# Order of work at three places of an encoder block: weights' splits behind the fourth row's norm, second product's operands behind the last group's first copy, and the last two rows' final norm

## The chip, the cores and the metric

The kernel runs on one core of a Trainium2 chip. The metric is device time of one execution in microseconds (us). Times of the trace are counted from the start of the span, the stretch that the profiler records.

## The reference

The input x is 1024 tokens by 1024 features, all in float32. What is computed:

```python
xn = _rmsnorm(h, norm_mix_w[l])
proj = xn @ w_in[l]                       # 1024 x 2832
...
h = h + jnp.concatenate([attn, gdn], axis=-1) @ w_out[l]
hn = _rmsnorm(h, norm_ffn_w[l])
h = h + jnp.square(jax.nn.relu(hn @ w_ffn_in[l])) @ w_ffn_out[l]   # 4096 inner columns
...
return _rmsnorm(h, norm_final_w)
```

`attn` is windowed attention of 8 heads, `gdn` a gated delta rule in both directions of 4 heads. The change touches the start (first norm and the first columns of `w_in`), the passage from the feed-forward block's first product to its second, and the final norm.

## The kernel before, in words

**Precision.** A float32 operand is split into two fp32r parts, hi and lo: ACT casts it to hi (L123, L1193), and POOL (L124) or DVE (L1194) subtracts hi from it for lo. A product is then three matmuls (`mm3`, L136 hi by hi, L137 hi by lo, L138 lo by hi). L numbers are lines of the kernel; in the changed kernel the same lines have numbers 1 or 2 higher from L214 on, and in the tail other ones, which are named where they matter.

**Buffers.** Tiles come from pools of a few rotating buffers, and the letters in front of a tile's name are its pool: `pg`, `dbl`, `pt`, `wr`, `wh`, `wl`, `sc` in SBUF, `psA` and `psB` of four banks each in PSUM. The numbers behind it (pt_8560) tell apart the tiles of a pool.

**Who sets the order.** Each engine works through one queue in order. The order in the queues is made when the program is built, by a scheduler that simulates the engines. Two instructions on different engines are tied by semaphores where one needs the other's data or buffer. `behind([...])` (L127) ties everything that is built in its scope to come after the given instructions in the queue of the engine that each of them is on; it adds no semaphore.

**Start.** For each row block of 128 tokens (`norm_rows`, L213 to L215) ACT squares and sums the row, POOL makes the reciprocal root in two steps (L200, L201), and DVE multiplies the row by it. PE transposes the first four blocks (L219); ACT and DVE scale the transposed parts by the norm's weight and split them (L224, L225). `proj_ab` casts a narrow weight (L291 on ACT, L292 on POOL, L293 and L296 on DVE) and gives PE its first real matmuls (L302, L303). The weights of the next projection `k` are split behind it (L123, L124).

**Feed-forward, first product.** It runs in 16 groups of 256 inner columns (`pair_products`). A group uses a scheme of seven products, P1 to P7, in place of eight; each is 12 matmuls of 128x512 here. P1, P6, P5, P7, P3, P4 share banks: P6 is accumulated onto P1's bank, after ACT has copied P1 out (L1106, `copied`); P3 onto P5's, after DVE has read that one (`add_to`, L1101); P4 onto P7's, after DVE has read that. Relu and Square are on ACT (L1111, L1112). DVE makes four sums of the results (L1162 to L1170), and all seven are stored to memory from ACT's queue (L1117).

**Second product.** It takes the same seven in the order of `SECOND`: P1, P2, P6, P5, P7, P3, P4, for each of four ranges of inner columns. `second_operands` prepares one: SP loads the left sides (L1192), ACT casts them (L1193) and DVE makes lo (L1194); of the weights DVE makes the sums T1, T2 (L1201, L1203), T3 and N4 (L1206, L1207), and ACT and POOL split them (L123, L124). In the last group the operands of the second product's first steps are prepared while the first product still runs: `prepare(0)` behind that group's P2, further ones behind P6 and P3, through `prepare_behind`:

```python
def prepare_behind(i):
    with self.behind(last_split):
        prepare(i)
```

`last_split` are the casts and subtractions of the last group's own weights, on ACT and POOL.

**Tail.** In the last range the rows are finished as P3 and P4 come out: `finish` squares a row on ACT (L1269), makes the reciprocal root on POOL and weighs the row on DVE by root and weight in one operation (L1272), then stores it (L1273). The last row, 7, is finished in halves by `finish_last` (L1253 to L1263): the upper half's Square and weighing (POOL, L1254) don't need the last matmuls, the lower half's do (L1255 to L1257).

Of the kernel before, what the change touches and what calls it, by code (L numbers as in the profile page):

```python
# [12 lines left out]
BF16 = mybir.dt.bfloat16  # L13
AF = mybir.ActivationFunctionType
ALU = mybir.AluOpType
AX = mybir.AxisListType

P = 128
# [50 lines left out]
def run(gen):  # L69
    for _ in gen:  # L70
        pass
# [7 lines left out]
class Block:  # L79
# [118 lines left out]
    def rstd(self, ss, out):  # L198
        nc = self.nc
        nc.gpsimd.tensor_scalar(out=ss, in0=ss, scalar1=1.0 / D, scalar2=EPS, op0=ALU.mult, op1=ALU.add)  # L200
        nc.gpsimd.tensor_tensor(out=out, in0=ss, in1=self.nhalf_exp[:, :1], op=ALU.pow)  # L201

    def load_x(self, t):
        x = self.pg((P, D))
# [3 lines left out]
    def norm_rows(self, x, dst=None):  # L208
        nc = self.nc
        ss, rs = self.small((P, 1)), self.small((P, 1))  # L210
        xs = dst if dst is not None else x
        scr = self.pt((P, D), BF16)
        nc.scalar.activation(out=scr, in_=x, func=AF.Square, accum_out=ss)  # L213
        self.rstd(ss, rs)  # L214
        nc.vector.tensor_scalar(out=xs, in0=x, scalar1=rs, scalar2=None, op0=ALU.mult)  # L215
        return xs

    def transpose_row(self, row, i, ps, k):
# [884 lines left out]

    def copied(self, ps):
        t = self.pt()
        self.nc.scalar.copy(out=t, in_=ps)  # L1106
        return t

    def act(self, c):
# [108 lines left out]
    def second_products(self, n, p, left, right, banks, last):  # L1218

        nc = self.nc  # L1220
        bank, tag = {"P1": ("a", "psA"), "P2": ("b", "psB"), "P5": ("c", "psB"), "P7": ("d", "psA"), "P6": ("a", None),
                     "P3": ("c", None), "P4": ("d", None)}[p]
        lo, hi = slice(0, HALF), slice(HALF, D)
        for i in range(4):
            ps = banks[bank, i] = self.ps(tag) if tag else banks[bank, i]
            tk = slice(i * P, (i + 1) * P)
            for k in range(4):
                self.mm3(ps, left[k][:, 0, tk], left[k][:, 1, tk], right[k][:, 0], right[k][:, 1],
                         tag is not None and k == 0, k == 3, tag is None)
            u2 = self.u2[i // 2][:, i % 2]  # L1230
            if p == "P6" and n == 0:
                nc.scalar.copy(out=u2, in_=ps)
                continue
            dst = {"P1": self.h[i][:, lo], "P2": self.h[i][:, lo], "P6": u2, "P5": self.h[4 + i][:, hi],
                   "P7": self.h[4 + i][:, hi], "P3": self.h[i][:, hi], "P4": self.h[4 + i][:, lo]}[p]
            if p == "P4" and last and i == 3:
                self.finish_last(7, ps)
                continue
            nc.vector.tensor_tensor(out=dst, in0=dst, in1=ps, op=ALU.add)  # L1239
            if last and p == "P6":  # L1240
                for d in (self.h[i][:, hi], self.h[4 + i][:, hi], self.h[4 + i][:, lo]):
                    nc.gpsimd.tensor_tensor(out=d, in0=d, in1=u2, op=ALU.add)
            if last and p in ("P3", "P4"):
                self.finish(i if p == "P3" else 4 + i)

    def finish_last(self, t, ps):

        nc = self.nc
        lo, hi = slice(0, HALF), slice(HALF, D)
        h = self.h[t]  # L1250
        ss, rs = self.small((P, 2)), self.small((P, 1))
        scr, hw, o = self.pt((P, HALF), BF16), [self.pt(), self.pt()], [self.pt(), self.pt()]
        nc.scalar.activation(out=scr, in_=h[:, hi], func=AF.Square, accum_out=ss[:, 1:2])  # L1253
        nc.gpsimd.tensor_tensor(out=hw[1], in0=h[:, hi], in1=self.w_fin[:, hi], op=ALU.mult)  # L1254
        nc.vector.tensor_tensor(out=h[:, lo], in0=h[:, lo], in1=ps, op=ALU.add)  # L1255
        nc.scalar.activation(out=scr, in_=h[:, lo], func=AF.Square, accum_out=ss[:, 0:1])
        nc.vector.tensor_tensor(out=hw[0], in0=h[:, lo], in1=self.w_fin[:, lo], op=ALU.mult)  # L1257
        nc.vector.tensor_tensor(out=ss[:, 0:1], in0=ss[:, 0:1], in1=ss[:, 1:2], op=ALU.add)
        self.rstd(ss[:, 0:1], rs)
# [2 lines left out]
        for i, sl in enumerate((lo, hi)):  # L1262
            (nc.scalar, nc.sync)[i].dma_start(out=self.io["out"][0, t * P:(t + 1) * P, sl], in_=o[i])  # L1263

    def finish(self, t):
        nc = self.nc
        ss, rs = self.small((P, 1)), self.small((P, 1))
        scr = self.pt((P, D), BF16)
        nc.scalar.activation(out=scr, in_=self.h[t], func=AF.Square, accum_out=ss)  # L1269
        self.rstd(ss, rs)  # L1270
        o = self.wr((P, D))
        nc.vector.scalar_tensor_tensor(out=o, in0=self.h[t], scalar=rs, in1=self.w_fin, op0=ALU.mult, op1=ALU.mult)  # L1272
        nc.sync.dma_start(out=self.io["out"][0, t * P:(t + 1) * P, :], in_=o)  # L1273

# [21 lines left out]
    def phases(self):  # L1296
# [11 lines left out]
        for half in range(2):  # L1308
            rows = [self.norm_rows(xs[4 * half + i]) for i in range(4)]
            self.xt.append([])  # L1310
            if half == 0:
                self.transpose_first(rows, self.w_mix, self.xt[half])
                next(ab)
            else:
                run(weave((itertools.islice(k, 2), 10.4),
                          (self.transpose_split(rows, self.w_mix, "psB", self.xt[half]), 4.0)))
                next(ab)
        run(ab)
        run(k)
# [45 lines left out]
            ops[i] = self.second_operands(n, w2[n], p)  # L1365

        def prepare_behind(i):
            with self.behind(last_split):
                prepare(i)

        def after_p6():
# [52 lines left out]
```

## Time and profile before

| what | value |
|---|---|
| median of 3 runs | 1226.01 us (1224.49 to 1228.44) |
| the profiled execution | 1226.09 us |
| its span | 1224.0 us |
| mean granted clock of PE | 0.989 |
| busy: PE, DVE, ACT, POOL | 96%, 70%, 50%, 46% of the span |
| DMA | 187.62 MB, mean 153 GB/s |

A row of the timeline gives the start, the duration, the engine, the line, the operation, the tile written and the tiles read, the shape, and the count where like rows are joined. In brackets stands how long the engine had been idle before it, and what ended that. PE's matmuls are pipelined: a row lasts longer than the step to the next one, and it is the steps that count. PE is the matmul, PEld the weight load beside it, SPq and ACTq are DMAs issued from those queues.

### The profile page before, as it was taken

How to read it: one execution, taken by the hardware profiler on the slowest of the kernel's cores; microseconds unless marked ns; L12 is line 12 of the kernel's file. 1: busy time of each engine (PE TensorE's matmuls, PEld its weight loads, DVE VectorE, ACT ScalarE, POOL GpSimd, SP SyncE). 2: the span in 40 equal slices, each digit the busy share in tenths (PEclk: the TensorE clock that was granted, in tenths of full speed). 3: DMA queues.
4: the chain of work that ended last, by engine and by line, in shares of the span. 5: the costliest groups of instructions: out<-in, count | busy, mean ns of one | idle time of the engine just before them, and what ended most of it. 6: DMA issues, size and time to landing. Idle time of an engine off the chain costs nothing. (4 is left out here: it accounts for less than half of the span.)

```text
span 1224.0 us, 18445 instructions
## 1 busy us (share of the span) xinstructions
PE 1173.7 (96%) x6482; PEld 961.9 (79%) x6482; DVE 855.7 (70%) x1482; ACT 610.4 (50%) x1331; POOL 560.2 (46%) x470
## 2 busy tenths in 40 slices
PE   6999999899889999998999999999999999999997
PEld 5788878687768878887788888888878888888885
DVE  4676667993489996675855454453698796987976
ACT  6455688425376662124755454554555444344443
POOL 5354312224321233232764453635456565565695
PEclk9999999899989999999999999999999999999999
DMA  6134344433645577222144444344789534343323
GB/s 244 52 103 145 92 170 152 162 123 113 207 146 182 157 249 269 76 95 100 56 154 157 146 154 164 130 155 146 240 275 317 200 103 163 131 159 116 103 86 138
DMA packets 121629, 187.62 MB, mean 153 GB/s; under 512 B 11043, under 2 KB 64416, under 8 KB 121537
## 3 DMA queue, kind: packets, MB, share of 16 engines
q1 hardware_dynamic: 103876, 155.20, 38.4%
q10 hardware_dynamic: 17661, 31.24, 6.8%
q8 instruction: 51, 0.84, 0.3%
q14 instruction: 41, 0.34, 0.1%
HBM read 122.39 MB, written 63.49 MB: 152 GB/s over the span
## 5 line engine op out<-in xcount | busy, mean ns | idle before, releaser
L136 PE MATMUL psA<-pg,wh 128*128 128x512 f32 x416 | 165.0, 397 | 2.1 <-ACT pt L473 2.1
L138 PE MATMUL psA<-pg,wl 128*128 128x512 f32 x416 | 164.5, 395 | 0.0
L137 PE MATMUL psA<-pg,wh 128*128 128x512 f32 x416 | 164.2, 395 | 0.0
L124 POOL TENSOR_TENSOR wl<-wr,wh 128x512 fp32r<-128x512 f32 x44 | 66.8, 1540 | 156.5 <-ACT wh L123 128.7
L1194 DVE TENSOR_TENSOR pg<-pg 128x512 fp32r<-128x512 f32 x112 | 124.3, 1145 | 12.9 <-ACT pg L1193 12.9
L124 POOL TENSOR_TENSOR wh<-wr,wh 128x512 fp32r<-128x512 f32 x32 | 47.0, 1487 | 138.2 <-ACT wh L123 138.2
L1111 ACT ACTIVATE pt<-pt 128x512 f32<-128x512 f32 x64 | 40.3, 632 | 122.6 <-DVE pt L1101 122.6
L136 PE MATMUL psA<-pg,pg 128*128 128x512 f32 x256 | 98.7, 391 | 0.9 <-DVE pg L1239 0.9
L137 PE MATMUL psA<-pg,pg 128*128 128x512 f32 x256 | 99.2, 391 | 0.1
L138 PE MATMUL psA<-pg,pg 128*128 128x512 f32 x256 | 99.2, 389 | 0.0
L136 PEld LDWEIGHTS psA<-pg,wh 128*128 128x128 f32 x416 | 78.8, 190 | 19.5 <-ACT pt L473 2.4
L137 PEld LDWEIGHTS psA<-pg,wh 128*128 128x128 f32 x416 | 78.7, 189 | 17.9 <-issue 0.9
L138 PEld LDWEIGHTS psA<-pg,wl 128*128 128x128 f32 x416 | 78.7, 189 | 16.7
L124 POOL TENSOR_TENSOR pg<-wr,pg 128x512 fp32r<-128x512 f32 x48 | 73.2, 1559 | 37.9 <-ACT pg L123 37.9
L1193 ACT CAST pg<-pg 128x512 fp32r<-128x512 f32 x112 | 66.7, 620 | 36.4 <-DMA pg<-sd 31.3
L137 PE MATMUL psB<-pg,pg 128*128 128x512 f32 x192 | 74.9, 390 | 0.8 <-POOL pg L124 0.7
L136 PE MATMUL psB<-pg,pg 128*128 128x512 f32 x192 | 74.7, 389 | 0.0
L138 PE MATMUL psB<-pg,pg 128*128 128x512 f32 x192 | 74.7, 389 | 0.0
L123 ACT CAST wh<-wr 128x512 fp32r<-128x512 f32 x76 | 43.6, 623 | 52.1 <-PE psA L137 31.9
L1101 DVE TENSOR_TENSOR pt<-psB,pt 128x512 f32<-128x512 f32 x39 | 26.9, 690 | 57.6 <-PE psB L138 40.7
L1101 DVE TENSOR_TENSOR pt<-psA,pt 128x512 f32<-128x512 f32 x39 | 26.7, 689 | 51.3 <-PE psA L138 34.1
L136 PEld LDWEIGHTS psA<-pg,pg 128*128 128x128 f32 x256 | 48.0, 188 | 12.1 <-DVE pg L1239 2.1
(395 smaller groups left out, 3234.8 us busy)
## 6 DMA issues: line engine op xcount, KB each, us to landing
sd<-pt ACTq DMA_DIRECT2D x112, 256.0 KB, 2.1
pg<-sd SPq DMA_DIRECT2D x112, 256.0 KB, 2.9
wr<-in_w_ffn_in SPq DMA_DIRECT2D x32, 512.0 KB, 3.6
wr<-in_w_in SPq DMA_DIRECT2D x22, 512.0 KB, 4.2
pg<-in_x SPq DMA_DIRECT2D x16, 512.0 KB, 5.0
wr<-in_w_ffn_out SPq DMA_DIRECT2D x16, 512.0 KB, 4.7
sc<-kvd SPq DMA_DIRECT2D x14, 512.0 KB, 3.7
kvd<-pt SPq DMA_DIRECT2D x16, 256.0 KB, 2.4
```

What stands on the lines that cost most here:

```text
L123: a = nc.scalar.copy(out=h, in_=raw)
L124: b = (eng or nc.gpsimd).tensor_tensor(out=l, in0=raw, in1=h.bitcast(F32), op=ALU.subtract)
L136: nc.tensor.matmul(ps, wh, xh, start=first, stop=False, skip_group_check=onto)
L137: nc.tensor.matmul(ps, wh, xl, start=False, stop=False, skip_group_check=onto)
L138: return nc.tensor.matmul(ps, wl, xh, start=False, stop=last, skip_group_check=onto)
L1101: self.nc.vector.tensor_tensor(out=out, in0=in0, in1=in1, op=ALU.add)
L1111: self.nc.scalar.activation(out=c, in_=c, func=AF.Relu)
L1193: nc.scalar.copy(out=s[:, 0], in_=raw)
L1194: v.tensor_tensor(out=s[:, 1], in0=raw, in1=s[:, 0].bitcast(F32), op=ALU.subtract)
```

## The change

There are three parts.

1. **Start.** `norm_rows` keeps its Square, its power and its multiplication (`self.normed`). Those of the fourth row block are what `proj_ab`'s first piece (its casts) and the first two pieces of the projection `k` (its weights' splits) are now built behind, on ACT, POOL and DVE.
2. **Last group.** `copied` keeps its copy (`self.moved`), and `prepare_behind` puts the preparation behind that as well: `prepare(0)` behind the copy of the last group's P1, the next ones behind the copy of its P6.
3. **Tail.** Row 7's upper half is squared and weighed (`finish_hi`) ahead of row 6's finish. Row 6 is weighed by the weight alone (L1288 of the changed kernel), and multiplied by its root later, on ACT behind the Square of row 7's lower half (L1270); its store is issued there.

```diff
     def norm_rows(self, x, dst=None):
...
+        s = nc.scalar.activation(out=scr, in_=x, func=AF.Square, accum_out=ss)
+        p = self.rstd(ss, rs)
+        m = nc.vector.tensor_scalar(out=xs, in0=x, scalar1=rs, scalar2=None, op0=ALU.mult)
+        self.normed = [s.ins, p, m.ins]
...
     def copied(self, ps):
         t = self.pt()
-        self.nc.scalar.copy(out=t, in_=ps)
+        self.moved = self.nc.scalar.copy(out=t, in_=ps).ins
...
+            if last and p == "P4" and i == 2:
+                self.finish_hi(7)
             if last and p in ("P3", "P4"):
-                self.finish(i if p == "P3" else 4 + i)
+                self.finish(i if p == "P3" else 4 + i, p == "P4" and i == 2)
+
+    def finish_hi(self, t):
+
+        nc = self.nc
+        hi = slice(HALF, D)
+        h = self.h[t]
+        self.fs, self.fhi, scr = self.small((P, 2)), self.pt(), self.pt((P, HALF), BF16)
+        nc.scalar.activation(out=scr, in_=h[:, hi], func=AF.Square, accum_out=self.fs[:, 1:2])
+        nc.gpsimd.tensor_tensor(out=self.fhi, in0=h[:, hi], in1=self.w_fin[:, hi], op=ALU.mult)
 
     def finish_last(self, t, ps):
...
         nc.vector.tensor_tensor(out=h[:, lo], in0=h[:, lo], in1=ps, op=ALU.add)
-        nc.scalar.activation(out=scr, in_=h[:, lo], func=AF.Square, accum_out=ss[:, 0:1])
+        square = nc.scalar.activation(out=scr, in_=h[:, lo], func=AF.Square, accum_out=ss[:, 0:1])
+        late, late_rs, late_t = self.late
+        with self.tc.issue_after(square.ins):
+            nc.scalar.activation(out=late, in_=late, func=AF.Copy, scale=late_rs)
+        nc.sync.dma_start(out=self.io["out"][0, late_t * P:(late_t + 1) * P, :], in_=late)
...
         o = self.wr((P, D))
+        if weigh_first:
+            nc.vector.tensor_tensor(out=o, in0=self.h[t], in1=self.w_fin, op=ALU.mult)
+            self.late = o, rs, t
+            return
...
             if half == 0:
+                first = self.normed
                 self.transpose_first(rows, self.w_mix, self.xt[half])
-                next(ab)
+                with self.behind(first):
+                    next(ab)
             else:
-                run(weave((itertools.islice(k, 2), 10.4),
-                          (self.transpose_split(rows, self.w_mix, "psB", self.xt[half]), 4.0)))
+                with self.behind(first):
+                    run(weave((itertools.islice(k, 2), 10.4),
+                              (self.transpose_split(rows, self.w_mix, "psB", self.xt[half]), 4.0)))
...
         def prepare_behind(i):
-            with self.behind(last_split):
+            with self.behind(last_split + [self.moved]):
                 prepare(i)
```

On ACT, in the last two groups, the queue before has these rows between group 14's last output (pt_8461 is its a12, the result of P4) and the copy of group 15's P1 out of bank psB_8546; the casts of the second product's P1 (pg_8578 to pg_8590) stand 20 to 23 rows ahead of it:

```order
L1112 ACTIVATE pt_8506<-pt_8506 128x512
L1111 ACTIVATE pt_8461<-pt_8461 128x512
L1112 ACTIVATE pt_8461<-pt_8461 128x512
L1193 CAST pg_8688<-pg_8688 128x512
L1117 DMA sd<-pt_8511 128x512
L1117 DMA sd<-pt_8461 128x512
L1117 DMA sd<-pt_8506 128x512
L1117 DMA sd<-pt_8512 128x512
L1106 COPY pt_8560<-psB_8546 128x512
L1193 CAST pg_8692<-pg_8692 128x512
```

At the same place of ACT's queue the changed kernel has:

```order
L1113 ACTIVATE pt_8461<-pt_8461 128x512
L1119 DMA sd<-pt_8506 128x512
L1114 ACTIVATE pt_8461<-pt_8461 128x512
L1119 DMA sd<-pt_8512 128x512
L1119 DMA sd<-pt_8461 128x512
L1108 COPY pt_8560<-psB_8546 128x512
L1195 CAST pg_8578<-pg_8578 128x512
L1195 CAST pg_8582<-pg_8582 128x512
```

The casts for the second product now all stand behind the copy; ahead of the copy there are still Relu and Square of group 14's last output and the stores.

On PE, behind the last matmuls of group 14's P4 (bank psA_8478), the kernel before has the second product's P1 (psA_8743 and three more banks), and P6 of group 15 (onto psB_8546) 42 matmuls later:

```order
L136 MATMUL psA_8478<-pg_6300,sc_8263 128x512
L137 MATMUL psA_8478<-pg_6300,sc_8263 128x512
L138 MATMUL psA_8478<-pg_6300,sc_8263 128x512
L136 MATMUL psA_8743<-pg_8594,pg_8578 128x512
L137 MATMUL psA_8743<-pg_8594,pg_8578 128x512
```

In the changed kernel P6 of group 15 follows at once (12 matmuls, then 31 of the second P1, P3 of group 15 onto psB_8634, 2 more, and P4 onto psB_8649):

```order
L136 MATMUL psA_8478<-pg_6300,sc_8263 128x512
L137 MATMUL psA_8478<-pg_6300,sc_8263 128x512
L138 MATMUL psA_8478<-pg_6300,sc_8263 128x512
L136 MATMUL psB_8546<-dbl_6237,sc_8402 128x512
L137 MATMUL psB_8546<-dbl_6237,sc_8402 128x512
```

The 42 matmuls that stood between P4 and P6 have moved behind P6.

On DVE the kernel before has the add that frees the bank of group 15's P3 (pt_8647<-psB_8634) behind lo parts of the second product; the sums T1 and T3 of the weights, but the last, are done 14 to 21 rows earlier:

```order
L1101 TENSOR_TENSOR pt_8560<-psB_8547,pt_8560 128x512
L1194 TENSOR_TENSOR pg_8692<-pg_8692 128x512
L1206 TENSOR_TENSOR wr_8544<-sc_8632,wr_8544 128x512
L1194 TENSOR_TENSOR pg_8696<-pg_8696 128x512
L1194 TENSOR_TENSOR pg_8700<-pg_8700 128x512
L1194 TENSOR_TENSOR pg_8799<-pg_8799 128x512
L1194 TENSOR_TENSOR pg_8803<-pg_8803 128x512
L1101 TENSOR_TENSOR pt_8647<-psB_8634,pt_8618 128x512
```

In the changed kernel DVE has, from the same first row to the same add (rows 1012 to 1022 of its queue):

```order
L1103 TENSOR_TENSOR pt_8560<-psB_8547,pt_8560 128x512
L1196 TENSOR_TENSOR pg_8578<-pg_8578 128x512
L1196 TENSOR_TENSOR pg_8582<-pg_8582 128x512
L1196 TENSOR_TENSOR pg_8586<-pg_8586 128x512
L1196 TENSOR_TENSOR pg_8590<-pg_8590 128x512
L1203 TENSOR_TENSOR wr_8538<-wr_8538 128x512
L1208 TENSOR_TENSOR wr_8538<-wh_8626,wr_8538 128x512
L1203 TENSOR_TENSOR wr_8540<-wr_8540 128x512
L1208 TENSOR_TENSOR wr_8540<-wl_8628,wr_8540 128x512
L1203 TENSOR_TENSOR wr_8542<-wr_8542 128x512
L1103 TENSOR_TENSOR pt_8647<-psB_8634,pt_8618 128x512
```

Four lo parts and five sums T1 and T3 (L1203, L1208) now stand between the two adds, each T1 behind POOL's split of the same weights (it overwrites them).

More of the change, by code (lines that the diff above doesn't have):

```diff
@@ L200, in rstd @@
         nc.gpsimd.tensor_scalar(out=ss, in0=ss, scalar1=1.0 / D, scalar2=EPS, op0=ALU.mult, op1=ALU.add)
-        nc.gpsimd.tensor_tensor(out=out, in0=ss, in1=self.nhalf_exp[:, :1], op=ALU.pow)
+        p = nc.gpsimd.tensor_tensor(out=out, in0=ss, in1=self.nhalf_exp[:, :1], op=ALU.pow)
+        return p.ins
     def load_x(self, t):
@@ L212, in norm_rows @@
         scr = self.pt((P, D), BF16)
-        nc.scalar.activation(out=scr, in_=x, func=AF.Square, accum_out=ss)
-        self.rstd(ss, rs)
-        nc.vector.tensor_scalar(out=xs, in0=x, scalar1=rs, scalar2=None, op0=ALU.mult)
+        s = nc.scalar.activation(out=scr, in_=x, func=AF.Square, accum_out=ss)
+        p = self.rstd(ss, rs)
+        m = nc.vector.tensor_scalar(out=xs, in0=x, scalar1=rs, scalar2=None, op0=ALU.mult)
+        self.normed = [s.ins, p, m.ins]
         return xs
@@ L1250, in finish_last @@
         h = self.h[t]
[L1251 to L1254, printed above, removed]
+        ss, rs = self.fs, self.small((P, 1))
+        scr, hw, o = self.pt((P, HALF), BF16), [self.pt(), self.fhi], [self.pt(), self.pt()]
         nc.vector.tensor_tensor(out=h[:, lo], in0=h[:, lo], in1=ps, op=ALU.add)
-        nc.scalar.activation(out=scr, in_=h[:, lo], func=AF.Square, accum_out=ss[:, 0:1])
+        square = nc.scalar.activation(out=scr, in_=h[:, lo], func=AF.Square, accum_out=ss[:, 0:1])
[3 more added lines that the diff above has]
+        nc.sync.dma_start(out=self.io["out"][0, late_t * P:(late_t + 1) * P, :], in_=late)
         nc.vector.tensor_tensor(out=hw[0], in0=h[:, lo], in1=self.w_fin[:, lo], op=ALU.mult)
@@ L1263, in finish_last, with finish @@
             (nc.scalar, nc.sync)[i].dma_start(out=self.io["out"][0, t * P:(t + 1) * P, sl], in_=o[i])
-    def finish(self, t):
+    def finish(self, t, weigh_first=False):
         nc = self.nc
```

## The prediction

> **What bounds the kernel now.** I read the engines' shares, then the list of what PE waits for (in total, times, longest), then the timelines of PE and ACT around the one of these waits that the change can reach, and of the start and the tail.
>
> ```profile
> PE 1173.7 (96%) x6482; PEld 961.9 (79%) x6482; DVE 855.7 (70%) x1482; ACT 610.4 (50%) x1331; POOL 560.2 (46%) x470
> ...
> PE psB L136 <- ACT pt L1106: 2.1, 1, 2.1
> ```
>
> PE is busy for 96% of the span, so the matmuls are the bound, and the change, which takes no matmul away, can only win or lose where PE stands still: the start, the one hole before L136 that ends with the ACT copy of L1106, and the tail. The profiled execution took 1226.09 us for its span of 1224.0; the median of the runs is 1226.01, so the sum below is made against 1226.1 for both. A measurement can tell about 0.3% from no change, 3.7 us: faster is below 1222.4, slower above 1229.8.
>
> The hole, in PE's timeline (start, duration), with ACT's row that ends it and the window of one us behind it (the granted clock is the third number from the end):
>
> ```profile
> 894.51 0.39 PE L138 MATMUL psA<-pg,sc 128*128 128x512 f32 x1
> 894.74 0.39 PE L136 MATMUL psA<-pg,pg 128*128 128x512 f32 x1
> ...
> 906.50 0.50 PE L136 MATMUL psB<-dbl,sc 128*128 128x512 f32 x1 [2.08 <-ACT pt L1106]
> ...
> 910.95 0.40 PE L136 MATMUL psA<-pg,pg 128*128 128x512 f32 x1
> ...
> 928.65 0.39 PE L136 MATMUL psA<-pg,pg 128*128 128x512 f32 x1
> ```
>
> ```profile
> 905.86 0.59 ACT L1106 COPY pt<-psB 128x512 f32<-128x512 f32 x1 [2.99 <-DVE pt L1164]
> ```
>
> ```profile
> 907.00:908.00 1.00, 1.00 (x5) 0.74 (x4) 1.00 (x3) 1.00 (x3) 0.00 (x0) 0.52 1.07 410
> ```
>
> The row at 894.51 is the last matmul of the first product's P4 in group 14. From 894.74 PE does 42 matmuls of the second product's P1 at 0.2267 us each (the step from 894.51 to 894.74), to 904.26, and then stands still 2.24 us until the copy is out of group 15's P1 bank, on which P6 accumulates. Behind that gap the granted clock falls to half (0.52): P6's 12 matmuls, to 910.95, take 4.45 us where 12 x 0.2267 = 2.72 would do, 1.73 lost. Check: from 894.74 to 928.65, where the second P6 starts, there are 132 matmuls; 132 x 0.2267 + 2.24 + 1.73 = 33.9, and the rows give 33.91. So this place costs 4.0 us now.
>
> **The change, part by part.** *Start*, on ACT, DVE and PE:
>
> ```profile
> 8.88 0.19 ACT L213 ACTIVATION_READ_ACCUMULATOR pt<-pg 128x1 f32 x1
> 9.64 0.30 ACT L291 CAST wh<-wr 128x128 fp32r<-128x128 f32 x1 [0.57 <-DMA wr<-in_w_in]
> 9.85 1.05 ACT L213 ACTIVATE pt<-pg 128x1024 bf16<-128x1024 f32 x1
> ...
> 12.34 1.14 ACT L123 CAST wh<-wr 128x512 fp32r<-128x512 f32 x2 [0.23 <-DMA wr<-in_w_in]
> 14.23 2.42 ACT L224 ACTIVATE pg<-psA,cols 128x512 fp32r<-128x512 f32 x4 [0.75 <-PE psA L219]
> ```
>
> ```profile
> 8.93 0.75 DVE L215 TENSOR_SCALAR pg<-pg,sm 128x1024 f32<-128x1024 f32 x1 [0.72 <-POOL sm L201]
> ...
> 12.06 1.75 DVE L215 TENSOR_SCALAR pg<-pg,sm 128x1024 f32<-128x1024 f32 x1 [0.72 <-POOL sm L201]
> ```
>
> ```profile
> 15.85 0.39 PE L302 MATMUL psA<-pg,wh 128*32 128x512 f32 x1 [0.89 <-DVE pg L225]
> ```
>
> The fourth Square (9.85) waits behind a cast whose load came at 9.64. Without it the Square starts at about 9.07, when the third one's read is over: 0.8 earlier. The fourth multiplication then starts at about 11.3 instead of 12.06 and, with POOL's splits behind it, takes 0.75 as the row at 8.93 does, not 1.75: it ends 1.8 earlier, near 12.0, and the transposes let L224 start up to 1.6 earlier (a little less, since the third row's now come closer before). But ACT's four weight casts still stand ahead of L224, and the second pair of them waits for its load at 12.34 and ends at 12.34 + 1.14 = 13.48. So L224 starts at 13.45 instead of 14.23: **-0.8 us**, and everything behind it as well, since PE has work from 15.85 on. Bounds: -1.6, if the transposes set it, and -0.3, if the casts of L291 and L293, now later themselves, hold back the first L302.
>
> *The last group.* The prepare steps (casts, splits and sums for the second product) now stand on ACT behind the first copy. The order around them shows that the copy isn't early for that: it stands behind the Square of group 14's last output (pt_8461), which needs P4 of that group, and PE has P6 directly behind that P4. What PE had to do in between is moved behind P6. The wait is issued on ACT; behind it are queued the casts, and DVE, POOL and PE wait for these.
>
> The price of the first wait comes from the same steps one group earlier, which stand in this order already:
>
> ```profile
> 876.39 0.39 PE L138 MATMUL psA<-pg,sc 128*128 128x512 f32 x1
> ...
> 879.44 0.59 ACT L1106 COPY pt<-psA 128x512 f32<-128x512 f32 x1 [0.52 <-ACT pt L1112]
> ```
>
> From the end of the P4 there (PE goes on at 876.39) to the end of the copy at 880.03 it takes 3.64 us: the add, Relu, Square, stores, copy. There PE had other matmuls; here it has none. So P6 starts at 894.74 + 3.69 = 898.43: a gap of 3.69, longer than the one it replaces, and I expect half clock behind it as behind that.
>
> Then come the operands, at the pace of DVE and POOL:
>
> ```profile
> 887.53 4.60 DVE L1194 TENSOR_TENSOR pg<-pg 128x512 fp32r<-128x512 f32 x3
> 892.05 1.77 DVE L1201 TENSOR_TENSOR wr<-wr 128x512 f32<-128x512 f32 x1
> ...
> 899.06 0.69 DVE L1206 TENSOR_TENSOR wr<-sc,wr 128x512 f32<-128x512 f32 x1
> ```
>
> ```profile
> 889.85 5.13 POOL L124 TENSOR_TENSOR pg<-wr,pg 128x512 fp32r<-128x512 f32 x3
> 895.99 1.28 POOL L124 TENSOR_TENSOR pg<-wr,pg 128x512 fp32r<-128x512 f32 x1 [1.02 <-ACT pg L123]
> ```
>
> ```profile
> 895.29 0.62 ACT L123 CAST pg<-wr 128x512 fp32r<-128x512 f32 x1 [4.77 <-DMA wr<-in_w_ffn_out]
> ```
>
> While both are at work, a DVE operation takes 1.53 to 1.77 and POOL's split 1.71; alone they take 0.69 and 1.28. So they go in turns, about 1.7 to a pair. Before, these turns lay between 887 and 895, under a PE that had work. Now they begin at about 901.4, when the first cast behind the copy is out (four casts of the left side first), and POOL has eight splits in a row, to 902.65 + 7 x 1.71 = 914.6. In DVE's row five sums (T1, T3, T1, T3, T1) stand ahead of the add that frees the bank of P3 in group 15 (pt_8647<-psB_8634): 902.65 + 5 x 1.7 = 911.2 to 911.5, and with the add 912.2. PE has 31 matmuls of the second P1 behind P6; four run at once, 27 need the first split: 902.65 + 27 x 0.2267 = 908.8. P3 waits from then to 912.2, 3.4 us (1.7, where half clock has delayed PE by 1.7: the end is the same). P3 takes 2.72 and two others 0.45: 915.35. P4 waits for the next add (pt_8647<-psB_8649), behind four more DVE operations, two of them in turns: 912.1 + 2 x 1.7 + 2 x 0.69 = 916.9. Then 12 + 15 + 48 = 75 matmuls, 17.0 us: the second P6 starts at 933.9 instead of 928.65, **+5.3**. Bounds: 4.6, if the sums begin 0.7 sooner, and 5.9, if P3's wait is put 0.6 later. I take +5.3, since each duration has a row. The loads that SP issues for this at other places I take at nothing: ACT waits for one in this stretch, until 895.29, and that operand is wanted after 900 now; one that came late would cost PE up to its own lateness.
>
> [...]
>
> *Tail*, on DVE and POOL, and the stores of one row (count, size, us from issue to landing):
>
> ```profile
> 1213.81 1.28 DVE L1272 SCALAR_TENSOR_TENSOR wr<-pg,sm,wl 128x1024 f32<-128x1024 f32 x1
> 1215.93 0.69 DVE L1255 TENSOR_TENSOR pg<-pg,psA 128x512 f32<-128x512 f32 x1 [0.84 <-PE psA L138]
> 1216.53 1.84 DVE L1272 SCALAR_TENSOR_TENSOR wr<-pg,sm,wl 128x1024 f32<-128x1024 f32 x1
> ```
>
> ```profile
> 1216.02 1.27 POOL L1254 TENSOR_TENSOR pt<-pg,wl 128x512 f32<-128x512 f32 x1
> ...
> 1219.40 0.55 POOL L201 TENSOR_TENSOR sm<-sm,nhalf_exp 128x1 f32<-128x1 f32 x1
> ```
>
> ```profile
> out<-wr SPq DMA_DIRECT2D x7, 512.0 KB, 2.6
> ```
>
> Row 6 is weighed without its rs and now ahead of row 7's last add; POOL's product for row 7 (1.27) moves beside row 5's weighing at 1213.81, which it holds up as it now does row 6's (1.84); so row 5 is weighed until about 1215.7 and row 6, in 1.28, until about 1216.9, and the add starts there instead of at 1215.93. Behind the add DVE has no 1.84 any more, and POOL no product. Square, weighing and the sum of squares follow at once, and POOL's last power ends at about 1219.45 instead of 1219.95: 0.5 earlier. But row 6's 512 KB leave only when ACT has multiplied them by rs, behind row 7's Square, at 1219.45 instead of 1218.4 (1216.53 + 1.84); with 2.6 us to land that is 1222.05, beside the last two stores. Bounds -0.5 (the chain alone) and +0.9 (the stores share the way); I take **0**, the two against each other.
>
> Sum: 1226.1 - 0.8 + 5.3 + 0 = 1230.6.
>
> **The rivals.** *No turns* (chance 0.20). If DVE gets through the five sums and the add at 0.69 each, the add is done by about 906.6, ahead of PE's 908.8, and only the first gap counts: 3.69 for 2.24, and half clock again or not. The last group then costs 3.69 + 1.73 - 3.97 = +1.5 with the spell; without it PE waits 0.6 for the first split, 3.69 + 0.6 - 3.97 = +0.3. The time is 1225.6 to 1226.8, no slower than before. For it: POOL's splits may come late from ACT, and then DVE is alone. Against: in 887 to 895 every operation of the two was in turns. It decides from an add that ends before 908.8. [...]
>
> *The whole hole goes* (0.12). If the copy ended before P4's matmuls did, PE would run through: 2.24 and 1.73 gained, 1226.1 - 0.8 - 4.0 = 1221.3, faster. For it: P1 of group 15, which the copy reads, is done long before. Against: the Square ahead of it on ACT, and the 3.64 above, which has three operations of 0.6 that can't be left out. It decides from a copy that ends before 895.
>
> *More spells* (0.13). The waits of 3.4 and 1.6 before P3 and P4, or second P6's operands, which the same DVE and POOL have to make by 933.9, bring another spell of half clock: +1.7, as the 1.73 above: 1232.3.
>
> **How the numbers follow.** My forecast has 0.55, with 1228.6 (all the low bounds) to 1232.6 (all the high ones) of its own; some three quarters of it are above 1229.8. Slower: 0.41 and the 0.13 of more spells, 0.54; within 0.3%: 0.14 and the 0.20 of no turns, 0.34; faster 0.12. The range goes from 1224.8, which takes in no turns with more gained at the start, to 1233.5, a further spell with part of the high bounds.
>
> **What would show it.** Right: PE idle some 3.7 us behind group 14's P4, ended by the copy; an idle time of 1.5 to 3.5 before group 15's P3, ended by DVE's add, with DVE's sums at 1.7 beside POOL; L302 near 15.1; the tail's span from the last matmul as before. Wrong: no idle time before that P3 (no turns), a copy that ends before 896 (the hole goes), or a second P6 that starts less than 3 us later against the group's start.

## The result and the profile after

| what | before | after |
|---|---|---|
| median of 16 runs each | 1227.57 us (1224.49 to 1232.53) | 1233.04 us (1229.09 to 1237.46) |
| ratio | | 1.005 (1.0039 to 1.0061): 6.1 us more (4.8 to 7.5) |
| the profiled execution, its span | 1226.09, 1224.0 us | 1236.67, 1234.9 us |
| granted clock of PE | 0.989 | 0.983 |

The change makes the kernel slower by 6.1 us, taken from the ratio (5.5 between the two medians), where the forecast had 4.5. The direction and the place are as forecast; the size isn't. The 1233.04 is 2.4 above the forecast of 1230.6: 1.5 of that is that the kernel before has a median of 1227.57 over 16 runs and not 1226.1. The rest, 0.9 by the medians and 1.6 by the ratio, is of the size of the errors in two terms of the sum, below.

The profiled execution is 3.6 us over its kernel's median, so the two traces can't simply be subtracted. Two windows of the changed kernel show why (the third number from the end is the granted clock):

```profile
272.00:273.00 1.00, 0.90 (x5) 0.66 (x4) 0.95 (x4) 0.96 (x3) 0.95 (x3) 0.69 1.02 391
...
608.00:609.00 1.00, 0.70 (x3) 0.54 (x3) 1.00 (x3) 1.00 (x3) 1.00 (x2) 0.50 0.00 0
```

The same windows of the kernel before:

```profile
272.00:273.00 1.00, 1.00 (x6) 0.83 (x5) 0.95 (x4) 0.96 (x3) 0.61 (x3) 1.00 1.10 367
...
608.00:609.00 1.00, 1.00 (x6) 0.84 (x5) 0.10 (x1) 1.00 (x3) 1.00 (x2) 1.00 0.00 0
```

PE falls behind by 1.7 us at the first place and 2.5 at the second, in code that the change doesn't touch. Of the 17 profiled executions of this case, 8 show half clock at the first place and 11 around the second, in kernels with and without the change's parts. So they are left out, and the two kernels are compared stretch by stretch, each from a PE row of its own.

**The last group.** The engines' shares on the changed kernel's page, and from its list of PE's waits (in total, times, longest) the two kinds that answer to the one of before:

```profile
PE 1180.4 (96%) x6482; PEld 966.4 (78%) x6482; DVE 853.7 (69%) x1482; ACT 611.5 (50%) x1332; POOL 561.0 (45%) x470
```

```profile
PE psB L136 <- ACT pt L1108: 3.9, 1, 3.9
...
PE psB L136 <- DVE pt L1103: 1.7, 2, 1.1
```

Where one wait of 2.1 stood there are now three, 5.6 in all. In PE's timeline:

```profile
900.18 0.39 PE L138 MATMUL psA<-pg,sc 128*128 128x512 f32 x1
904.50 0.79 PE L136 MATMUL psB<-dbl,sc 128*128 128x512 f32 x1 [3.93 <-ACT pt L1108]
...
917.98 0.50 PE L136 MATMUL psB<-pg,wl 128*128 128x512 f32 x1 [0.55 <-DVE pt L1103]
...
922.57 0.50 PE L136 MATMUL psB<-pg,sc 128*128 128x512 f32 x1 [1.12 <-DVE pt L1103]
...
939.74 0.39 PE L136 MATMUL psA<-pg,pg 128*128 128x512 f32 x1
```

The row at 900.18 is the last of group 14's P4; the next matmul could have started at 900.41, where 894.74 stood before. Counted from there, P6 starts at 4.09, P3 at 17.57, P4 at 22.16 and the second P6 at 39.33; the forecast, 898.43, 912.2, 916.9 and 933.9 less 894.74, had 3.69, 17.5, 22.2 and 39.2. Before it was 33.91: +5.42 between the two profiled executions, as forecast (+5.3). ACT's copy ends the first gap, and the window of one us behind it has half clock:

```profile
903.87 0.58 ACT L1108 COPY pt<-psB 128x512 f32<-128x512 f32 x1 [0.94 <-DVE pt L1172]
```

```profile
906.00:907.00 1.00, 1.00 (x4) 0.81 (x3) 1.00 (x3) 1.00 (x4) 0.00 (x0) 0.50 1.05 406
```

What holds P3 and P4 is in DVE's timeline:

```profile
908.76 1.75 DVE L1203 TENSOR_TENSOR wr<-wr 128x512 f32<-128x512 f32 x1 [1.18 <-POOL pg L124]
910.54 1.67 DVE L1208 TENSOR_TENSOR wr<-wh,wr 128x512 f32<-128x512 f32 x1
912.13 1.79 DVE L1203 TENSOR_TENSOR wr<-wr 128x512 f32<-128x512 f32 x1
913.96 1.67 DVE L1208 TENSOR_TENSOR wr<-wl,wr 128x512 f32<-128x512 f32 x1
915.54 1.77 DVE L1203 TENSOR_TENSOR wr<-wr 128x512 f32<-128x512 f32 x1
917.24 0.68 DVE L1103 TENSOR_TENSOR pt<-psB,pt 128x512 f32<-128x512 f32 x1
```

Five sums at 1.7 beside POOL's splits, and then the add that frees P3's bank. The half clock behind the first gap takes 3.0 of PE's time, not the 1.7 that the prediction reckoned with: 43 matmuls from 904.50 would end at 914.25 at full clock and end at 917.26. It costs nothing of its own, since the add is only out at 917.92: the start of P3 is set by DVE in either case, and only the wait before it is shorter, 0.55.

**The start.** DVE, ACT and PE of the changed kernel:

```profile
12.19 1.09 DVE L216 TENSOR_SCALAR pg<-pg,sm 128x1024 f32<-128x1024 f32 x1 [0.71 <-POOL sm L201]
13.20 1.29 DVE L295 CAST wh<-wh 128x128 fp32r<-128x128 f32 x1
14.41 1.30 DVE L298 CAST wh<-zab 128x128 fp32r<-128x128 f32 x1
15.64 2.71 DVE L227 SCALAR_TENSOR_TENSOR pg<-psA,cols,pg 128x512 fp32r<-128x512 f32 x4
```

```profile
13.75 2.42 ACT L226 ACTIVATE pg<-psA,cols 128x512 fp32r<-128x512 f32 x4
```

```profile
8.59 1.12 PE L221 MATMUL psA<-ident,pg 128*128 128x128 f32 x4 [8.59 <-DVE pg L216]
...
16.52 0.39 PE L304 MATMUL psA<-pg,wh 128*32 128x512 f32 x1 [2.04 <-DVE pg L227]
```

Counted from the first transposes (8.59; 8.26 in the kernel before, whose first x row came earlier), ACT's scaling starts at 5.16 instead of 5.97: the 0.8 of the forecast. But DVE's two casts for the narrow weight now stand behind the fourth multiplication too, beside POOL's splits, and hold its L227 back to 15.64. So the first L304 comes at 7.93 instead of 7.59: **+0.34**, not -0.8. The cast of the zeros (L298 here, L296 in the kernel before) had been done at 1.80 before.

**The tail.** DVE and POOL behind PE's last matmul, which is at 1226.47:

```profile
1226.51 1.21 DVE L1288 TENSOR_TENSOR wr<-pg,wl 128x1024 f32<-128x1024 f32 x1
1227.64 0.67 DVE L1266 TENSOR_TENSOR pg<-pg,psA 128x512 f32<-128x512 f32 x1
```

```profile
1229.63 0.55 POOL L201 TENSOR_TENSOR sm<-sm,nhalf_exp 128x1 f32<-128x1 f32 x1
```

The last power ends 3.71 us behind the last matmul instead of 4.45, but the span ends 8.43 behind it instead of 8.50. The 0.7 that the chain gains doesn't reach the end: 0, as forecast. Row 6's store is now issued at 1230.14, just ahead of the last two, and from the issue of the last one (1230.96; 1220.74 in the kernel before) to the end of the span it takes 3.9 instead of 3.3. That is the forecast's "two against each other"; that the stores share the way was not measured by itself.

### The profile page after: what moved, and what is told of

Read it like the earlier page. It is cut to its first block, busy times and chain, and to the rows that moved or that the text cites. A ratio compares the mean times of both kernels' runs of the same rounds, so it can differ in the third digit from the quotient of the medians.

```text
span 1234.9 us, 18448 instructions
## 1 busy us (share of the span) xinstructions
PE 1180.4 (96%) x6482; PEld 966.4 (78%) x6482; DVE 853.7 (69%) x1482; ACT 611.5 (50%) x1332; POOL 561.0 (45%) x470
## 5 line engine op out<-in xcount | busy, mean ns | idle before, releaser
L1196 DVE TENSOR_TENSOR pg<-pg 128x512 fp32r<-128x512 f32 x112 | 121.0, 1113 | 13.9 <-ACT pg L1195 13.9
L1103 DVE TENSOR_TENSOR pt<-psA,pt 128x512 f32<-128x512 f32 x39 | 26.7, 689 | 56.9 <-PE psA L138 39.2
```

The costliest lines, as they stand in the source:

```text
L1103: self.nc.vector.tensor_tensor(out=out, in0=in0, in1=in1, op=ALU.add)
L1196: v.tensor_tensor(out=s[:, 1], in0=raw, in1=s[:, 0].bitcast(F32), op=ALU.subtract)
```

## The experiments

A measure that all of them share is the **stretch**: from PE's first free slot behind group 14's P4 to the start of P5 in the second product's first range. 180 matmuls lie in it, 40.8 us at 0.2267 each; the rest is waits and half clock. It is 45.04 in the profile of the kernel before and 50.43 in that of the changed one. The ratio behind each time is to the kernel before on the same chip; from one group of runs to another only the ratios compare.

**The three parts, each alone: e1_start_only, e2_group_only, e3_tail_only.** Each is the change's diff for its part, put into the kernel before; of each a line or two:

```diff
+                first = self.normed
...
+                with self.behind(first):
+                    next(ab)
```

```diff
-            with self.behind(last_split):
+            with self.behind(last_split + [self.moved]):
```

```diff
+            if last and p == "P4" and i == 2:
+                self.finish_hi(7)
```

> The start's part alone, on the kernel before. Theory (two DVE casts, now behind the fourth multiplication and beside POOL's splits, 1.3 us each, stand ahead of the lo part of the transposed rows, so the 0.8 us that ACT wins are lost again): L304's first matmul starts 8.0 us or more behind the first transpose (before: 15.85 - 8.26 = 7.59; the changed kernel: 16.52 - 8.59 = 7.93), and the time is +0.0 to +0.8 us, a ratio of 1.000 to 1.001. My prediction's term: -0.8 us, L304 6.8 us behind the first transpose. Rival (the start also moves where half-clock spells fall later on, and these make most of the slowdown): +2 us or more, 1.002 and above.

> The last group's part alone. Theory (the copy behind the Square leaves PE idle, then half clock, then DVE's sums in turns with POOL hold the adds): from the first slot behind group 14's P4 to the second P6 it takes 39.3 us (before 33.9), the time is +5.0 to +5.8 us, a ratio of 1.0041 to 1.0047. Rival (half-clock spells elsewhere make a large part): the stretch takes 39.3 all the same, but the time is +3 us or less, 1.0025 or below.

> The tail's part alone. Theory: the last power ends 0.7 us earlier against the last matmul, the store of row 6 leaves some 1.5 us later, and the end of the span against the last matmul stays within 0.3 us of the 8.50 us before: ratio 0.9995 to 1.0005. Rival (the stores of row 6 and row 7 share the way and set the end): +0.5 us or more behind the last matmul.

Measured: start alone 1227.51 against 1227.49, ratio 1.000 (0.9989 to 1.0011); group alone 1232.28, 1.0038 (1.0022 to 1.0054); tail alone 1226.34, 0.9992 (0.9978 to 1.0005). So the last group is what makes the change slower, by 4.7 us (2.7 to 6.6). Two of the three waits of the kernel with that part alone, in PE's timeline:

```profile
898.10 0.79 PE L136 MATMUL psB<-dbl,sc 128*128 128x512 f32 x1 [3.72 <-ACT pt L1106]
...
911.59 0.50 PE L136 MATMUL psB<-pg,wl 128*128 128x512 f32 x1 [0.87 <-DVE pt L1101]
```

Its stretch is 50.19. The start alone shows the casts again, in DVE's timeline:

```profile
12.33 1.29 DVE L295 CAST wh<-wh 128x128 fp32r<-128x128 f32 x1
13.54 1.30 DVE L298 CAST wh<-zab 128x128 fp32r<-128x128 f32 x1
```

Its first L304 is at 15.65, 7.94 behind the first transposes (7.71). The tail alone ends 8.51 behind its last matmul.

**The start without DVE's casts in the way: e4_start_free_dve.** The cast of the zeros is built ahead of the norms, and nothing is queued behind the multiplication on DVE, so that its other cast goes early too.

```diff
+        zero = self.small((P, NK * 16), bufs=1, tag="zab")
+        nc.gpsimd.memset(zero, 0.0)
+        nc.vector.tensor_copy(out=whz[:, :, 16:32], in_=zero.rearrange("p (k c) -> p k c", k=NK))
+        yield
         nc.scalar.copy(out=whl[:, :, 0:16], in_=raw)
...
+                first = self.normed[:2]
```

> The start's part, but DVE's casts are free: the zeros' cast is built ahead of the norms and the other cast isn't queued behind the fourth multiplication (ACT and POOL are queued as in the change). Theory: the lo part starts as soon as ACT's hi part lets it, L304's first matmul 6.6 to 7.0 us behind the first transpose (before 7.59), time -0.6 to -1.0 us, ratio 0.9992 to 0.9995. Rival (the transposes or the weights' casts on ACT hold L304, not DVE): 7.5 us or more and no gain.

Its DVE and PE:

```profile
10.78 0.22 DVE L299 CAST wh<-wh 128x128 fp32r<-128x128 f32 x1
...
13.84 0.75 DVE L227 SCALAR_TENSOR_TENSOR pg<-psA,cols,pg 128x512 fp32r<-128x512 f32 x1 [1.31 <-ACT pg L226]
```

```profile
14.74 0.39 PE L305 MATMUL psA<-pg,wh 128*32 128x512 f32 x1 [0.89 <-DVE pg L227]
```

The first matmul of `proj_ab` comes 6.77 behind the first transposes (7.97) instead of 7.59: in this execution the 0.8 that the change was forecast to win is there, once the two casts don't stand in DVE's queue. The other four kernels with this start have 7.21 (e8), 7.36 (e9), 7.38 (e12) and 6.88 (e15), so what it wins is 0.2 to 0.8. Of the ten kernels with the start of before, eight have 7.58 to 7.74, two as much as the change's 7.93 or more (e13 7.93, e7 8.51). That the change wins nothing is thus plain; that it loses 0.34 rests on two executions. The time of e4 is 1226.1, ratio 0.999 (0.9972 to 1.0008), too little to be told from none.

**The copy first: e5_copy_first and e6_group_copy_first.** The end of group 14 (the add of its last output a12, Relu, Square, the last sum and their stores, kept as `pending`) is built behind the copy of group 15's P1, in the preparation of before (e5) and of the change (e6, with the line of e2 as well).

```diff
         p1 = self.copied(a)
+        if then:
+            with self.behind([self.moved]):
+                self.pending()
```

> The kernel before, with one other order: Relu, Square and stores of group 14's last output are built behind the copy of group 15's P1, so that ACT makes the copy ahead of them; the preparation stays where it was. Theory (the hole and its half clock are the whole price of the late copy): the copy ends before PE is through with the matmuls ahead of P6, P6 waits under 0.4 us, no half clock there, and from the first slot behind group 14's P4 to the second P6 it takes 29.9 to 30.6 us (before 33.9); time -3.3 to -4.0 us, ratio 0.9967 to 0.9973. Rival (a wait takes the hole's place: the adds that free the banks of P3 and P4, or the second P6's operands, are now what is late): the hole is gone, but the stretch still takes 32.5 us or more.

> The last group's part of the change with the copy early: preparation behind the copy as in the change, and the copy ahead of Relu, Square and stores of group 14's last output. Theory (of the 5.4 us the first gap and its half clock are most, since the copy was late; the turns of DVE and POOL are the rest and stay): P6 waits 1.0 to 1.5 us, no half clock, P3 and P4 of group 15 wait 2 to 4 us together for DVE's adds, the stretch takes 35 to 36.5 us (before 33.9, the change 39.3), time +1.0 to +2.6 us. Rival (it is the preparation behind the copy that costs, wherever the copy is): 38.5 us or more.

Measured: 1231.85, 1.0049 (1.003 to 1.0067), and 1230.57, 1.0042 (1.0028 to 1.0056). In e5 the hole before the first P6 shrinks to 0.89 without half clock, and two other waits come, before and in the second P6:

```profile
929.69 1.20 PE L136 MATMUL psA<-pg,pg 128*128 128x512 f32 x4 [1.36 <-ACT pg L123]
933.10 0.77 PE L137 MATMUL psA<-pg,pg 128*128 128x512 f32 x1 [2.22 <-POOL pg L124]
```

with half clock behind the second; its stretch is 47.73, longer than before. T2 (L1213 there), from which ACT and POOL make that operand, stands on DVE 31.2 us behind the free slot, as it did before: it is behind group 15's last results in DVE's queue, and PE only gets there sooner. In e6 the first gap is 1.39, no half clock, and P4 waits 2.39 for DVE's add instead, with half clock behind that; its stretch is 47.91, 2.3 better than the 50.19 of e2 and still longer than before. So in the profiles 2.3 of that part's cost hang on the late copy. The runs' times don't show it: +5.1 us for e6 (3.4 to 6.9), +4.7 for e2 (2.7 to 6.6).

**DVE's sums behind the adds: e7_group_sums_late.**

```diff
-            a22 = self.act(self.add_to(d, w))
+            self.add_to(d, w)
+            self.freed = self.added
+            a22 = self.act(w)
...
+            with self.behind(last_split + [self.moved] + ([self.freed] if i > 1 else [])):
```

> The last group's part of the change, with DVE's sums T1 and T3 and the rest of those two preparations built behind the add that frees the bank of group 15's P4. Theory (the sums in turns with POOL hold the adds): P3 and P4 wait under 0.4 us together for DVE (0.7 + 1.3 in the changed kernel), the first gap stays at 3.9 to 4.1 with its half clock, and the stretch takes 36.8 to 37.8 us instead of 39.3. Rival (the adds wait for something else, the copy of u2 on ACT or PE's own order): P3 and P4 still wait 1.5 us or more, 39 us. Second rival: the waits go and come back ahead of the second P6, whose operands need T1: 39 us.

Measured: 1233.37, 1.006 (1.0048 to 1.0073). The waits before P3 and P4 are gone, and the second P6 starts at 35.46 instead of the 39.09 of e2. But there PE waits for POOL's splits, four times, 2.1 in all, the longest of them:

```profile
935.40 0.50 PE L137 MATMUL psA<-pg,pg 128*128 128x512 f32 x1 [0.73 <-POOL pg L124]
```

Its stretch is 49.61, only 0.6 less than that of e2: what is won before P3 and P4 is lost again behind the second P6.

**Start and tail mended, and the copy first: e8_all_mended; without the copy: e9_start_free_tail.** Edits as in e4 and e3, and in e8 that of e5:

```diff
+                first = self.normed[:2]
...
+                self.finish_hi(7)
```

```diff
+                self.pending()
```

> The start's part with DVE's casts free, the tail's part as in the change, and for the last group the early copy without moving the preparation. Theory: the sum of the parts, -0.8 + 0 - 3.3 to -4.0 = -4.1 to -4.8 us, ratio 0.9961 to 0.9967. Rival (parts hide one another): -3 us or less gained.

> The start's part with DVE's casts free and the tail's part as in the change; the last group as before. Theory (the two add up, the tail gives nothing): L305's first matmul 6.8 us behind the first transpose, the end of the span 8.5 us behind the last matmul, time -0.5 to -1.2 us, ratio 0.9990 to 0.9996. Rival (what the start wins is lost again at a later wait for a load or for half clock): ratio 0.9998 to 1.0005.

Measured: e8 1231.02, 1.0045 (1.0033 to 1.0057), with waits of 3.06 and 2.20 at the second P6 and half clock there, stretch 50.33; e9 1225.35, 0.9992 (0.9975 to 1.0008). In e9 the order of the last group is that of before. Its hole, and the window behind it:

```profile
906.16 0.50 PE L136 MATMUL psB<-dbl,sc 128*128 128x512 f32 x1 [1.51 <-ACT pt L1109]
```

```profile
907.00:908.00 1.00, 1.00 (x6) 0.83 (x5) 1.00 (x2) 1.00 (x3) 0.00 (x0) 1.00 1.04 356
```

The clock stays at 1.00 and the stretch is 43.99, not 45.04. e1 (43.78), e3 (44.29) and e4 (43.77), which have this order too, also have no half clock there. So the 1.73 in the profile of before is not a fixed price of the order; the last section shows on what it hangs. Nor is the whole of it won where it is missing. These four then wait 0.5 to 1.0 in the second P6 for POOL, where the kernel before has no wait:

```profile
928.92 0.50 PE L137 MATMUL psA<-pg,pg 128*128 128x512 f32 x1 [0.64 <-POOL pg L124]
```

This row is that of e1. The four stretches are 0.8 to 1.3 shorter than that of before.

**T2 sooner: e10, e11, e12.** T2 is written over T1, and N4 made at once, so that T2 needn't wait for a `pt` buffer; T1 is made again for P5. e11 adds the copy first, e12 also the edits of e9.

```diff
-                b["T2"] = self.pt()
+                b["T2"] = b["T1"]
                 v.tensor_tensor(out=b["T2"], in0=b["B22"], in1=b["T1"], op=ALU.subtract)
+                b["N4"] = b["B21"]
+                v.tensor_tensor(out=b["N4"], in0=b["B21"], in1=b["T2"], op=ALU.subtract)
```

> The kernel before with one edit: the sum T2 of the second product's P6 is written over T1 and N4 is made with it at once, and T1 is made anew for P5 (4 more sums on DVE per range), so that T2 needs none of the 12 pt tiles and DVE has it some 20 us earlier. Theory (from the first slot behind group 14's P4 to the second P5 PE is held by the chain T2 - cast - split, not by the hole alone): no wait for POOL at the second P6, and the stretch to the second P5 takes 42.3 to 43.2 us where runs of that order took 43.8 to 44.3 without half clock; time -0.5 to -1.5 us. Rival (the hole alone holds it): 43.5 us or more, no gain.

> The early copy of group 15's P1 together with T2 in place. Theory (with the early copy alone the hole went and came back as a wait for T2's splits and half clock; with T2 early there is nothing left): P6 waits under 1 us, no wait at the second P6, the stretch to the second P5 takes 40.8 to 42.0 us (47.7 with the early copy alone, floor 180 matmuls x 0.2267 = 40.8), time -1.8 to -3.0 us, ratio 0.9975 to 0.9985. Rival (loads of the stored results, which were late with the early copy, hold DVE all the same): 44 us or more, no gain.

> All of it: start with DVE's casts free, tail as in the change, early copy, T2 in place. Theory: the sum of the parts, -0.8 + 0 - 1.8 to -3.0 = -2.6 to -3.8 us, ratio 0.9969 to 0.9979. Rival (the parts hide one another): ratio 0.9985 or more.

Measured: 1239.32, 1.0095 (1.0073 to 1.0116); 1230.84, 1.0033 (1.0017 to 1.005); 1232.08, 1.0041 (1.0019 to 1.0063). In e10 the sums now stand ahead of operations on DVE that free PSUM banks. In PE's timeline:

```profile
909.92 0.79 PE L136 MATMUL psA<-pg,pg 128*128 128x512 f32 x1 [3.49 <-DVE pt L1101]
...
926.44 0.77 PE L136 MATMUL psA<-pg,pg 128*128 128x512 f32 x1 [5.53 <-DVE dbl L1241]
```

In e11 the second P6 has no wait left, but a wait of 3.32 for DVE's add comes 11.6 behind the free slot, with 6.8 us at half clock; e12 has one of 3.04 there. The stretches are 55.73, 47.32 and 47.37.

**T2 at places between: e13, e14, e15.** In the first range alone, T2 stands behind the add of group 15's first output, N4 behind that of P7. e14 adds the copy first, e15 also the edits of e9.

```diff
+                if n == 0:
+                    b["T2"], b["N4"] = b["T1"], b["B21"]
+                    with self.behind([self.freed[0]]):
+                        v.tensor_tensor(out=b["T2"], in0=b["B22"], in1=b["T1"], op=ALU.subtract)
+                    with self.behind([self.freed[1]]):
+                        v.tensor_tensor(out=b["N4"], in0=b["B21"], in1=b["T2"], op=ALU.subtract)
```

> The kernel before with T2 in place for the first range only, queued on DVE behind the add of group 15's first output; N4 behind the add that frees group 15's P4. Theory (the old hole of 1.6 us and behind it T2's chain are all that holds PE here): the hole stays at 1.5 to 2.3 us, no wait at the second P6, and from the first slot behind group 14's P4 to the second P5 it takes 42.3 to 43.0 us (43.8 to 44.3 before, without half clock; floor 40.8), time -0.8 to -1.8 us. Rival (T2's sums hold another add, as they did when they were first): a new wait for DVE of 1 us or more, 43.8 us or more.

> The same with the early copy. Theory: the hole under 1 us, no wait at the second P6, 41.0 to 42.0 us to the second P5 (47.7 with the early copy alone), time -1.5 to -3.0 us, ratio 0.9975 to 0.9988. Rival (late loads of the stored results, or an add held by T2's sums, hold PE): 43.5 us or more and no gain.

> The same with the start's part with DVE's casts free and the tail's part. Theory: the sum, -2.3 to -3.8 us, ratio 0.9969 to 0.9981; the stretch as in the run before it. Rival (the start's 0.8 us is lost again at a later wait): the same ratio as that run.

Measured: 1227.82, 1.0012 (0.9999 to 1.0026); 1226.76, 1.0002 (0.9991 to 1.0014); 1225.09, 0.9995 (0.9983 to 1.0006). In e14 the hole of before is all but gone, and two others have come:

```profile
905.32 0.50 PE L136 MATMUL psB<-dbl,sc 128*128 128x512 f32 x1 [0.25 <-ACT pt L1106]
...
915.45 0.50 PE L138 MATMUL psB<-pg,pg 128*128 128x512 f32 x1 [1.37 <-DVE pg L1208]
...
929.03 0.50 PE L136 MATMUL psB<-pg,pg 128*128 128x512 f32 x1 [1.35 <-DVE pt L1101]
```

The stretches are 44.89, 45.14 and 43.97. Of what was expected, e1, e3 and e4 came out, and e2 in its stretch, with a time 0.3 under its bound; e9 came out in its time, but its start is at 7.36 instead of 6.8. In e5, e7, e13 and e14 a wait took the place of the one removed, which the rivals named (in e13 it is for POOL, not for DVE). e6, e8, e10, e11, e12 and e15 are misses: e6 is slower than expected, and the other five, expected to be faster than the kernel before, are the same or slower. None of the 15 kernels beats the one before by more than its interval; e3, e4, e9 and e15 point at 0.6 to 1.2 us less by their ratios, unproven.

## Why the prediction was right and wrong

- **The gap behind group 14's P4**: right. Forecast 3.69, measured 4.09, 3.88 in e2: the copy stands behind add, Relu, Square and stores, and PE has nothing else.
- **The turns of DVE and POOL, and the starts of P3 and P4**: right. The sums take 1.67 to 1.79 beside POOL, and P3, P4 and the second P6 come within 0.2 of the forecast. *No turns* falls with that. The wait before P3 is not in the forecast's 1.5 to 3.5: it is 0.55 (0.87 in e2), since the half clock, named by the prediction at 1.7, took 3.0 out of it.
- **The price of the old place, "this place costs 4.0 us now"**: wrong, by 1.0 in the sum. The 1.73 of half clock were read from one execution and taken for lasting. In four other executions of the same order the wait is 1.5 to 1.7, the clock stays at 1.00, and the stretch is 43.77 to 44.29 (mean 43.96) instead of 45.04. The forecast of the changed stretch (39.2 + 48 x 0.2267 = 50.0) was good, with 50.43 and 50.19 measured (mean 50.3); what it was taken from was too long. The group's part is 50.3 - 44.0 = +6.3 us, not +5.3; with the spell in one of five executions it is +6.1. That the two profiles differ by 5.4, as forecast, is no proof of the +5.3: the forecast took its price from this very profile. How often the kernel before has the spell was not measured, and e2's time (2.7 to 6.6) allows each of these.
- **The start, "-0.8 us" with bounds of -1.6 and -0.3**: wrong, by 1.1. What was moved on ACT came out (0.8 earlier), but the same `behind` moved two casts on DVE past the fourth multiplication, and beside POOL they take 1.29 and 1.30 instead of 0.23 and 0.51. The prediction named the casts of L291 and L293, but as a bound of -0.3 that still was a gain, and left out that of L296; it had no reason to exclude a loss, and asked what POOL's splits do to the fourth multiplication, not to what follows it. e1 and e4 show it: 7.94 with the casts there, 6.77 without (up to 7.38 in other kernels), 7.59 before. Beside them POOL's splits take 1.36 each (5.42 for four); ahead of the splits, in e4, the first of the casts takes 0.22. Why a cast is that much longer beside them was not measured by itself. The add that reads PSUM takes 0.68 at 917.24, with a split of POOL's beside it from 916.73, and 0.69 at 904.48, where POOL has nothing.
- **The tail, 0**: right. The chain ends 0.7 sooner, the span doesn't.
- **The whole hole goes**, with its price of -4.0: fell as a course of the change, and its price falls too. e5 takes half of the hole away and e14 nearly all of it, and the waits come back at other places (2.22 in the second P6; 1.37 and 1.35 in the second product's P2). No kernel's stretch is under 43.7. That DVE's and POOL's work for the second product sets this is what all these waits have in common; it was not measured by itself.
- **More spells**: not as the rival had it; the waits before P3 and P4 (0.55 and 1.12) and the second P6 bring none. Half clock does come at other places of the changed kernel, 272 and 608, but in kernels without its parts there as well (e5 and e14, for both).

Sum by what was measured: +0.34 + 6.3 + 0 = +6.6, beside 6.1 (4.8 to 7.5). The three parts alone, 0.0, +4.7 and -1.0 us by their ratios, add up to 3.7 with intervals of 1.3 to 2 us each, which is less; what lies between isn't settled beyond these intervals.

## What to carry to other kernels

Read the price of a place from more than one execution before taking it as what a change can win or lose, above all where a spell of half clock is in it: the wait may be the order's, while the spell hangs on where the wait falls. When a tie in the order moves a step, list its instructions on every engine and price each by its new neighbours: a cast of 0.2 us was 1.3 beside another engine's splits. And an idle time that ends with one copy needn't be free to take: here each of the ways to shorten it brought the wait back where the next operand or the next free bank was late.

## What the runs showed of the hardware

In this stretch PE's clock stayed at 1.00 behind every gap with a wait of up to 1.7 us (e1, e3, e4, e9, e13, and the 1.37 and 1.35 of e14), and fell to half behind each wait of 2.08 or more (before 2.08; e5 2.22; e6 2.39; then 3.0 to 5.5), but in e8, where it was still 1.00 behind the 3.06 and fell at 931.14, in the 2.20 that follows. The length of the wait is not all of it. In the clock records of all 17 profiles the spells of one execution start a whole number of steps of 3.413 us apart (within 0.002 us), and last one, two or three such steps (3.41, 6.83, 10.24), but for the last, which runs into the end of the kernel. Where the steps' edges fall differs from execution to execution. Here are windows cut at these edges, first of the kernel before around its hole, then of e9, whose P6 starts as far behind the free slot (11.78; 11.76 before) but which lost 0.6 of that in an earlier step. The second time in a line is PE's busy time:

```profile
903.63:907.04 3.41, 1.33 (x6) 0.82 (x5) 3.41 (x5) 1.18 (x3) 1.28 (x1) 1.00 0.86 225
907.04:910.45 3.41, 3.41 (x9) 2.64 (x8) 2.63 (x5) 2.96 (x6) 1.33 (x1) 0.50 1.04 388
```

```profile
903.76:907.17 3.41, 1.90 (x8) 1.25 (x8) 3.41 (x6) 1.65 (x4) 0.21 (x1) 1.00 0.98 266
907.17:910.58 3.41, 3.41 (x16) 2.82 (x15) 2.40 (x5) 2.96 (x6) 1.71 (x1) 1.00 1.03 386
```

In e1, e3 and e4 an edge lies within the hole, and neither step has PE busy for less than 2.46. At the place around 605 the edges make the same difference between e1 and the kernel before:

```profile
598.65:602.07 3.42, 1.58 (x13) 1.13 (x11) 3.42 (x6) 3.42 (x7) 3.16 (x3) 1.00 0.22 76
602.07:605.48 3.41, 2.90 (x8) 2.21 (x9) 3.41 (x7) 3.32 (x8) 3.41 (x4) 0.50 0.00 0
```

```profile
599.84:603.26 3.42, 2.31 (x16) 1.69 (x14) 3.42 (x6) 3.10 (x6) 2.75 (x3) 1.00 0.43 138
603.26:606.67 3.41, 1.69 (x9) 1.34 (x10) 3.41 (x6) 3.32 (x7) 3.41 (x4) 1.00 0.00 0
```

The kernel before is idle for longer there, but the edge divides that time, and no half clock follows. From 300 to 1205 us in all 17 profiles, full clock gives way to half clock 53 times, and each time PE was idle for at least 0.54 of the step ahead. Of the steps at full clock that no half clock follows, one has more than 0.53 (0.57, e7, near 560). So of the 17 executions the 11 with half clock around 605 have a step of 0.54 or more there, and the 6 without have none over 0.51. The place at 272 doesn't follow this: half clock comes there behind an idle share of 0.17 (the changed kernel), and not behind 0.46 (e6); why stays open.

A wait as long as the step was not needed: the kernel before has half clock behind 2.08, and the least idle share of the 53 is 0.54. And a spell can begin within the gap, at the edge of a step; a window of e10 in which PE stands still, and the next:

```profile
908.00:909.00 1.00, 0.00 (x0) 0.00 (x0) 1.00 (x3) 0.00 (x0) 0.00 (x0) 0.76 0.00 0
909.00:910.00 1.00, 0.08 (x1) 0.08 (x1) 1.00 (x3) 0.33 (x1) 0.00 (x0) 0.50 0.00 0
```
